# Neighbourhood attention: two heads' value products side by side in the array, and what moves with them

## The chip, the cores and the metric

The kernel runs on one core of a Trainium2 chip. The metric is the device time of one execution in microseconds (us); the kernel before has a median of 3476.13 us over three runs.

## What is computed

Two blocks run one after the other on 512 tokens of width 1024, with a context of 256 tokens. The change touches the first layer of the first block, which is a neighbourhood attention with 16 heads of 64 columns: a grid of 8 rows by 64 columns, where each token looks at a window of 8 by 16 neighbours and at all context tokens. Cut to that part:

```
q, k, v = split(h @ w_qkv)                   # q and k normalised per head
s = concat(q . k_window + bias, q . k_ctx)   # one head, one token
p = softmax(s)
o = p_window . v_window + p_ctx . v_ctx
x = x + g1 * (o @ w_o)                       # g1 and five more rows come from silu(c) @ ada_w + ada_b
x = x + g2 * swiglu(norm(x))                 # the feed-forward stage
```

The tokens of the context go through the same attention over the context alone. The layer after it is a gated scan, and two hybrid layers follow; the change leaves them as they are, except that rows for them are computed during the feed-forward stages.

## The kernel before

**The attention** is `na_heads` (L658). The work on one head is cut into six cells: four of 128 tokens (b = 0 to 3, with 512 scores for each token: 256 from the window, 256 from the context) and two of the context's tokens (b = 4 and 5, 256 scores). A hand-written order, fixed on TensorE (PE) and VectorE (DVE), takes one step g per cell: scores of cell g+1 (`na_scores`, L964), the transposes of the probabilities of cell g-1 (`na_turn`, L1003), the minimum of cell g+1 with the bias added (`na_max`, L981 and L983), its exponential on ScalarE (ACT; `na_exp`, L988), the values of cell g-2 (`na_values`, L1029), the copy of the transposed probabilities of cell g-1 out of PSUM (`na_copy`, L1013 and L1015), and the reciprocal of the sum of cell g+1 (`na_scale`, L994). The store of cell g-3 (`na_store`, L1036) multiplies by that reciprocal on the way from PSUM to `oT`. The cells run head by head: six cells of head 0, then six of head 1.

A value product takes the transposed probabilities `pT` (128 keys by 128 tokens) as the loaded operand and 64 columns of V as the moving one, so that `po` is 128 tokens by 64 columns. It is in float32, and the trace shows two records of PE (and two weight loads, PEld) for each such product. Elsewhere a product is written as three of split parts (`mm3`, L146 to L148), with one record each.

Between the cells PE is fed by a list of units: the projections for Q, K and V (`pacc`), and the transposes that follow for Q and K (`ptq`, L922). The list is paced so that the projections end at step 75 of 96 (`NA_STEPS`). From there to step 95 only the last of the jobs for the modulation rows are left, and this stretch is called the tail here.

**The modulation rows** (`gemv_rows`, L443): each job reads two blocks of `ada_w` (`araw`, 512 KB each) and multiplies them by the two condition vectors in four groups of 32 columns of the array (L464: four products at a time, each with 2 loaded columns, into PSUM rows 0, 32, 64 and 96). ACT copies the sums to `modx` (L468), a DMA of SyncE (SP) then lays the row of biases into partition 2 of `modx` (L469), and a last product with `sel` adds the groups and the bias (L475). The jobs are spread over the list of units; eleven of sixteen end in the tail.

**Behind the loop**, `split_rows` (L938) turns `oT` by 48 transposes on PE (L944), and ACT and DVE write it as a high and a low part, which `out_product` multiplies by `w_o` (`pw`, L146 to L148, 512 columns each). In the function `split_rows` is called for seven of the eight pairs of heads at g = 84 to 90.

**The feed-forward stages** (`ffn`, L286) walk over 22 blocks f. Each has its products (`pau`, `pc`), then silu on ACT, `g` on DVE (L335 and L338), and the parts `gh` on ACT (L341) and `gl` on DVE (L342). After 4, 4, 4, 4, 3 and 3 blocks comes a group of output products (`po`, L146 to L148) which read `gh` and `gl`. Rows for later layers are computed beside it on DVE (`gacc`, L430 to L435, nine long instructions for each vector of a job). There are 24 jobs in each of the two stages, two are begun behind each f, and their instructions are given a late priority, by which a scheduler mixes them into DVE's order.

The order within PE and DVE in the attention loop is the written one; all other engines, and work from outside the loop, are placed by the scheduler where its model has them ready. Every engine runs its queue in order.

Of the kernel before, what the change touches and what calls it, by code (L numbers as in the profile page):

```python
# [284 lines left out]
def ffn(S, l, xs, xout, more):  # L285
# [14 lines left out]
    every = (len(jobs) + 18) // 19  # L300
# [22 lines left out]
    for gi, gn in enumerate(groups):  # L323
        gts = []
        for f in range(f0, f0 + gn):
            pa, pu, *pc = dense(f)
            out_mm = S.lastmm
            g = fp.tile([128, n], F32, name="g", tag="g", bufs=2)
            sa = fp.tile([128, n], F32, name="sa", tag="sa", bufs=2)
            nc.scalar.activation(sa[:, 0:512], pa, AF.Silu)  # L330
            if l == 0:
                gv = g[:, 0:512].rearrange("p (r c) -> p c r", r=ROWS)
                nc.vector.tensor_mul(gv, *[x.rearrange("p (c r) -> p c r", r=ROWS) for x in (sa[:, 0:512], pu)])
            else:
                nc.vector.tensor_mul(g[:, 0:512], sa[:, 0:512], pu)  # L335
            if nt == 6:
                nc.scalar.activation(sa[:, 512:768], pc[0][:, 0:256], AF.Silu)
                nc.vector.tensor_mul(g[:, 512:768], sa[:, 512:768], pc[0][:, 256:512])  # L338
            gh = fp.tile([128, n], F32R, name="gh", tag="gh", bufs=7)
            gl = fp.tile([128, n], F32R, name="gl", tag="gl", bufs=7)  # L340
            nc.scalar.activation(gh, g, AF.Copy)  # L341
            nc.vector.tensor_sub(gl, g, fr(gh))  # L342
            gts.append((gh, gl))
            gemv_flush(S, fp, ps, ("gv", 1), out_mm.ins)
            S.late = late
            for j in jobs[:every]:
                jobs.pop(0)()
# [95 lines left out]
def gemv_rows(S, wname, layer, parts):  # L443
# [9 lines left out]
    sel = S.sb.tile([128, 2], F32, name="sel4")  # L453
    nc.vector.tensor_reduce(sel, S.idf.rearrange("p (j v) -> p v j", j=4)[:, 0:2, :], axis=AX.X, op=OP.add)
    nc.vector.tensor_add(sel, sel, S.idf[:, 2:3].to_broadcast([128, 2]))
    todo = []

    def half(part, c, h):
        S.mark(f"gemv {part}{layer}")
        c0 = PARTS[wname].index(part) * D + c * 256  # L460
        raw = S.gvpool.tile([128, 4, 256], F32, name="araw", tag="araw", bufs=2)
        nc.sync.dma_start(raw, S.wcols(w, c0, 256, 4 * h, 4))
        for k in range(4):
            nc.tensor.matmul(pg[32 * k:32 * k + 2, 0:256], S.cc[:, 4 * h + k, :], raw[:, k, :], start=(h == 0),  # L464
                             stop=(h == 1))
        if h:
            x = S.gvpool.tile([128, 256], F32, name="modx", tag="modx", bufs=1)
            nc.scalar.activation(x, pg[:, 0:256], AF.Copy)  # L468
            nc.sync.dma_start(x[2:3, :], bias[layer:layer + 1, c0:c0 + 256])  # L469
            todo.append((part, c, x))  # L470

    def total():
        part, c, x = todo.pop(0)
        S.mark(f"gemv {part}{layer}")
        nc.tensor.matmul(pg[0:2, 256:512], sel, x, start=True, stop=True)  # L475
# [182 lines left out]
def na_heads(S, na, hT, jobs):  # L658
# [13 lines left out]
    both = na.tile([128, 768], F32, name="bias")  # L672
    nc.gpsimd.memset(both[:, 256:512], 0.0)
# [35 lines left out]
    cells = [(h, b) for h in range(16) for b in range(6)]  # L709
    st = {}  # L710
    fill(NA_HEAD)
    with S.tc.manual_schedule(engines=NA_ENG):
# [8 lines left out]
        for g in range(-1, 100):  # L721
# [3 lines left out]
            if cell(g + 1):  # L725
                h, b = cells[g + 1]
                assert S.nturn[h // 2] == 12, (g, h)
                if b == 0:
                    wide = na.tile([128, 384], F32, name="wide", tag="wide", bufs=2)
                    nc.sync.dma_start(wide, I["rpb_w"][h])  # L730
                    st["wide"] = wide
                st[g + 1] = {}
                na_scores(S, na, st, g + 1, h, b, QK[h // 2][h % 2], mask)
            if cell(g - 3):
# [4 lines left out]
            if cell(g + 1):  # L739
                na_max(S, st[g + 1], *cells[g + 1])  # L740
            upto(g + NA_S[1])
            if cell(g + 1):
                na_exp(S, st[g + 1], *cells[g + 1])
            if cell(g - 2):
                h = cells[g - 2][0]
                assert cells[g - 2][1] or len(V[h // 4][1]) == 3, g
                na_values(S, st[g - 2], *cells[g - 2], V[h // 4])
# [5 lines left out]
            if cell(g + 1):  # L753
                na_scale(S, st[g + 1])
# [181 lines left out]

def split_rows(S, oR, oT, pr):
# [3 lines left out]
    for ts, (hi, lo) in ((range(4), oR.row(pr)), (range(4, 6), oR.crow(pr))):  # L941
        pt = S.acc(128 * len(ts))
        for i, t in enumerate(ts):
            nc.tensor.transpose(pt[:, i * 128:(i + 1) * 128], oT[t][:, pr * 128:(pr + 1) * 128], S.idf)  # L944
        nc.scalar.activation(hi, pt, AF.Copy)
        nc.vector.tensor_sub(lo, pt, fr(hi))


def na_scores(S, na, st, g, h, b, qk, mask):
# [16 lines left out]
    me.update(s=s, p=S.t2("p", n), mx=sb.tile([128, 4], F32, name="mx", tag="mx", bufs=7))  # L966
    if lat:
        if b == 0 or BVAR[b] != BVAR[b - 1]:
            S.bias.reverse()
            o = BOFF[b] * 8  # L970
            nc.gpsimd.tensor_sub(S.bias[0][0], mask[:, BVAR[b], :], st["wide"][:, o:o + 256])
        me["bias"] = S.bias[0][1]
# [18 lines left out]
def na_scale(S, me):  # L991
    S.mark("attscale")
    r = me["mx"][:, 3:4]
    S.nc.vector.reciprocal(r, r)  # L994

# [22 lines left out]
def na_values(S, me, h, b, V):  # L1018
    nc = S.nc
    S.mark(f"att{h}.{b}")  # L1020
    vc = (h % 4) * 64
# [765 lines left out]
```

## Time and profile before

| | us |
|---|---|
| median of three runs | 3476.13 |
| the three runs | 3475.0, 3476.13, 3479.37 |
| the profiled execution | 3472.26 |
| its span | 3470.5 |
| attention loop, projections still running | 109 to 420 of the span |
| the tail | 420 to 521 |
| feed-forward stages | about 600 to 1160, and 1680 to 2060 |

In the rows below PE, PEld, DVE, ACT, POOL and SP are the engines (PEld is PE's weight load). A record's first column is its start in us from the span's start, the second its length; the last bracket tells how long the engine stood idle before it, and what ended that. Ends of PE's records are modelled and overlap, so a product's price is read from one start to the next. PEclk is the clock that the throttle granted to PE, 1.00 being 2.4 GHz and 0.5 being 1.2 GHz.

### The profile page before, as it was taken

The numbers are of one execution on the slowest core, as the hardware profiler recorded it, in microseconds if no ns is written. First come the engines' busy times: TensorE is split into PE (matmuls) and PEld (weight loads), VectorE is DVE, ScalarE is ACT, GpSimd is POOL, SyncE is SP. The second block draws the span as 40 slices with busy tenths as digits, with TensorE's granted clock in tenths as the row PEclk, the third lists the DMA queues.
The fourth block names the chain that finished last, engine by engine and source line by source line (L and its number), as shares of the span: only waits on it lengthen the run. The fifth ranks groups of instructions, "written<-read, shape, count | busy, mean of one in ns | idle before, by whom it ended". The sixth has DMA issues, their size and how long they took to land.

```text
span 3470.5 us, 49643 instructions
## 1 busy us (share of the span) xinstructions
PE 3355.7 (97%) x18924; PEld 2838.8 (82%) x18924; DVE 1892.7 (55%) x3745; ACT 1259.4 (36%) x2480; POOL 720.1 (21%) x650
## 2 busy tenths in 40 slices
PE   7999989999999999999999999999999999999999
PEld 5999857887788788888777878888888788888887
DVE  6456544649864556578778544435552334355523
ACT  4455533222222433334422334333333343333332
POOL 2122202111111211101322223121222221211222
PEclk9999989999999999999999999999999999999999
DMA  6122244324531121111556434232223432322333
GB/s 202 49 75 67 63 135 141 97 67 128 176 116 56 54 62 44 55 49 49 163 165 195 119 108 125 80 104 73 92 78 101 144 104 80 110 69 91 94 97 100
DMA packets 450206, 345.30 MB, mean 99 GB/s; under 512 B 40336, under 2 KB 421552, under 8 KB 449968
## 3 DMA queue, kind: packets, MB, share of 16 engines
q1 hardware_dynamic: 449536, 341.73, 32.9%
q8 instruction: 148, 2.42, 0.3%
q0 software_dynamic: 432, 0.41, 0.1%
q14 instruction: 90, 0.74, 0.1%
HBM read 328.34 MB, written 12.74 MB: 98 GB/s over the span
## 4 chain that ended last, share of the span: by engine, by line
PE 74%; DVE 7%; DMA 2%; ACT 2%; issue 1%; POOL 1%; DVEq 0%; SPq 0%; POOLq 0%; ACTq 0%
PE pacc L148 12%; PE pacc L147 12%; PE pacc L146 12%; PE pau L148 3%; PE pau L146 3%; PE pau L147 3%; PE po L146 3%; PE po L148 3%; PE po L147 3%; PE pw L148 2%; PE pw L146 2%; PE pw L147 2%; DVE gacc L432 2%; PE pl L1194 2%; DVE wlo L135 1%
## 5 line engine op out<-in xcount | busy, mean ns | idle before, releaser
L135 POOL TENSOR_TENSOR wlo<-wraw,whi 128x512 fp32r<-128x512 f32 x388 | 526.7, 1359 | 2121.9 <-ACT whi L132 1762.1
L132 ACT ACTIVATE whi<-wraw 128x512 fp32r<-128x512 f32 x776 | 485.2, 631 | 796.9 <-PE pacc L147 357.8
L135 DVE TENSOR_TENSOR wlo<-wraw,whi 128x512 fp32r<-128x512 f32 x388 | 332.1, 857 | 552.1 <-ACT whi L132 547.4
L148 PE MATMUL pacc<-hT,wlo 128*128 128x512 f32 x1344 | 535.1, 398 | 0.0
L146 PE MATMUL pacc<-hT,whi 128*128 128x512 f32 x1344 | 534.6, 398 | 0.0
L147 PE MATMUL pacc<-hT,whi 128*128 128x512 f32 x1344 | 532.0, 396 | 0.0
L146 PE MATMUL pacc<-whi,hT 128*128 128x256 f32 x1056 | 307.4, 291 | 5.0 <-DVE h L607 2.9
L148 PEld LDWEIGHTS pacc<-hT,wlo 128*128 128x128 f32 x1344 | 252.8, 188 | 58.3
L147 PEld LDWEIGHTS pacc<-hT,whi 128*128 128x128 f32 x1344 | 252.7, 188 | 57.7
L147 PE MATMUL pacc<-wlo,hT 128*128 128x256 f32 x1056 | 299.4, 284 | 0.2 <-DVE wlo L813 0.2
L148 PE MATMUL pacc<-whi,hT 128*128 128x256 f32 x1056 | 298.4, 283 | 0.0
L146 PEld LDWEIGHTS pacc<-hT,whi 128*128 128x128 f32 x1344 | 253.0, 188 | 54.7
L146 PE MATMUL pau<-hT,whi 128*128 128x512 f32 x704 | 280.0, 398 | 0.7 <-DVE h L607 0.7
L148 PE MATMUL pau<-hT,wlo 128*128 128x512 f32 x704 | 280.2, 398 | 0.0
L147 PE MATMUL pau<-hT,whi 128*128 128x512 f32 x704 | 279.1, 396 | 0.0
L432 DVE SCALAR_TENSOR_TENSOR gacc<-araw,cact,gacc 128x256 f32<-128x256 f32 x392 | 222.0, 566 | 23.8 <-DMA araw<-ada_w 10.6
L146 PEld LDWEIGHTS pacc<-whi,hT 128*128 128x128 f32 x1056 | 200.5, 190 | 7.7 <-DVE h L607 3.1
L147 PEld LDWEIGHTS pacc<-wlo,hT 128*128 128x128 f32 x1056 | 200.9, 190 | 2.0 <-DVE wlo L813 0.4
L148 PEld LDWEIGHTS pacc<-whi,hT 128*128 128x128 f32 x1056 | 200.4, 190 | 0.0
L146 PE MATMUL po<-whi,gh 128*128 128x512 f32 x440 | 177.7, 405 | 17.0 <-ACT gh L341 15.7
L147 PE MATMUL po<-wlo,gh 128*128 128x512 f32 x440 | 175.6, 400 | 0.0
L148 PE MATMUL po<-whi,gl 128*128 128x512 f32 x440 | 175.1, 400 | 0.1
(375 smaller groups left out, 6600.4 us busy)
## 6 DMA issues: line engine op xcount, KB each, us to landing
araw<-ada_w SPq DMA_DIRECT2D x96, 512.0 KB
wraw<-w_in SPq DMA_DIRECT2D x96, 512.0 KB
wraw<-ffn_w_in SPq DMA_DIRECT2D x176, 256.0 KB
wraw<-w_in SPq DMA_DIRECT2D x160, 256.0 KB
araw<-w_ada SPq DMA_DIRECT2D x48, 512.0 KB
wraw<-ffn_w_out SPq DMA_DIRECT2D x40, 512.0 KB
x<-x SPq DMA_DIRECT2D x24, 512.0 KB
wraw<-hg_w_in SPq DMA_DIRECT2D x24, 512.0 KB
```

The source lines that it names most:

```text
L132: nc.scalar.activation(hi, r, AF.Copy)
L135: eng.tensor_sub(lo, r, fr(hi))
L146: nc.tensor.matmul(out, lh[0], rh[0], start=first, stop=False)
L147: nc.tensor.matmul(out, lh[0], rh[1], start=False, stop=False)
L148: self.lastmm = nc.tensor.matmul(out, lh[1], rh[0], start=False, stop=last)
L432: nc.vector.scalar_tensor_tensor(acc, r, cv, acc, op0=OP.mult, op1=OP.add)
L1194: nc.tensor.matmul(pl[:, c, :], KX[:, c * 128:(c + 1) * 128], view(Q, c * 128, ([2 * m, 64 // m], [LAT + m, 2], [1, m])), start=True, stop ...
```

## The change

1. `na_values` takes two heads at a time, the same block b of heads 2p and 2p+1. Now 64 columns of V are the loaded operand and `pT` the moving one (128 columns), and the two heads' results go to rows 0 to 63 and 64 to 127 of one `po`. This is called every second step. The result is already turned, so that `split_rows` needs no transposes and no PSUM.
2. Since the tokens are now columns, the division can't be done at the store. `na_scale` multiplies the probabilities themselves, in place, a step later than the reciprocal stood (cell g in step g, behind the minimum of g+1). `na_store` becomes a plain copy of 128 by 128, once for two cells.
3. The cells run in the order head 2p block b, head 2p+1 block b. Each of the two heads has a bias buffer of its own.
4. In `gemv_rows` the bias row goes to partition 98 of `modx`, which ACT's copy (rows 0 to 97) doesn't touch; its DMA is issued before the job's blocks are read.
5. In `ffn` the 24 jobs are spread evenly over 20 of the 22 blocks, instead of two behind each of the first twelve.

```diff
-    every = (len(jobs) + 18) // 19
+    njobs = len(jobs)
...
-            for j in jobs[:every]:
+            while jobs and (njobs - len(jobs)) * 20 < njobs * (f + 1):
                 jobs.pop(0)()
...
+    m = 3 * 32 + 2
...
+        if h == 0:
+            x = S.gvpool.tile([128, 256], F32, name="modx", tag="modx", bufs=1)
+            nc.sync.dma_start(x[m:m + 1, :], bias[layer:layer + 1, c0:c0 + 256])
+            todo.append((part, c, x))
...
         if h:
-            x = S.gvpool.tile([128, 256], F32, name="modx", tag="modx", bufs=1)
-            nc.scalar.activation(x, pg[:, 0:256], AF.Copy)
-            nc.sync.dma_start(x[2:3, :], bias[layer:layer + 1, c0:c0 + 256])
-            todo.append((part, c, x))
+            nc.scalar.activation(todo[0][2][0:m, :], pg[0:m, 0:256], AF.Copy)
...
-        nc.tensor.matmul(pg[0:2, 256:512], sel, x, start=True, stop=True)
+        nc.tensor.matmul(pg[0:2, 256:512], sel[0:m + 1, :], x[0:m + 1, :], start=True, stop=True)
...
-    cells = [(h, b) for h in range(16) for b in range(6)]
+    cells = [(2 * pr + i, b) for pr in range(8) for b in range(6) for i in range(2)]
...
-            if cell(g - 3):
+            if cell(g - 3) and g % 2 == 0:
+                st.pop(g - 4)
                 na_store(S, st.pop(g - 3), *cells[g - 3], oT)
...
                 na_max(S, st[g + 1], *cells[g + 1])
+            if cell(g):
+                na_scale(S, st[g])
...
-            if cell(g - 2):
+            if cell(g - 2) and g % 2:
...
-                na_values(S, st[g - 2], *cells[g - 2], V[h // 4])
+                na_values(S, [st[g - 3], st[g - 2]], *cells[g - 2], V[h // 4])
...
-            if cell(g + 1):
-                na_scale(S, st[g + 1])
...
-    for ts, (hi, lo) in ((range(4), oR.row(pr)), (range(4, 6), oR.crow(pr))):
-        pt = S.acc(128 * len(ts))
-        for i, t in enumerate(ts):
-            nc.tensor.transpose(pt[:, i * 128:(i + 1) * 128], oT[t][:, pr * 128:(pr + 1) * 128], S.idf)
-        nc.scalar.activation(hi, pt, AF.Copy)
-        nc.vector.tensor_sub(lo, pt, fr(hi))
+    for lat, (hi, lo) in ((True, oR.row(pr)), (False, oR.crow(pr))):
+        nc.scalar.activation(hi, o_row(oT, pr, lat), AF.Copy)
+        nc.vector.tensor_sub(lo, o_row(oT, pr, lat), fr(hi))
...
     S.nc.vector.reciprocal(r, r)
+    S.nc.vector.tensor_scalar(p, p, r, None, op0=OP.mult)
...
-    po = S.ps.tile([128, 64], F32, name="po", tag="pv", bufs=1)
+    po = S.ps.tile([128, 128], F32, name="po", tag="pv", bufs=1)
     for j, v in enumerate(vv):
-        nc.tensor.matmul(po, me["pT"][:, j, :], v[:, vc:vc + 64], start=(j == 0), stop=(j == len(vv) - 1))
-    me["po"] = po
+        for i, me in enumerate(two):
+            nc.tensor.matmul(po[64 * i:64 * i + 64, :], v[:, vc + 64 * i:vc + 64 * i + 64], me["pT"][:, j, :],
+                             start=(j == 0), stop=(j == len(vv) - 1))
+    two[1]["po"] = po
...
-    S.nc.vector.tensor_scalar(oT[b][:, h * 64:(h + 1) * 64], me["po"], me["mx"][:, 3:4], None, op0=OP.mult)
+    S.nc.vector.tensor_copy(o_row(oT, h // 2, b < 4)[:, (b % 4) * 128:(b % 4 + 1) * 128], me["po"])
```

PE's queue in the tail, before: `pg<-modx` is the last product of a job, `pg<-araw` one of its two halves, `s`, `pt` and `po` are scores, transposes and values of a cell, and `pacc<-idf,oT` the transposes of `split_rows`.

```order
L944 MATMUL pacc<-idf,oT 128x128 x6
L475 MATMUL pg<-modx,sel_477 2x256
L964 MATMUL s<-qk 128x512 x2
L1003 MATMUL pt<-idf,p 128x128 x4
L464 MATMUL pg<-araw,cc 2x256 x4
L1029 MATMUL po<-v,pT 128x64 x4
L944 MATMUL pacc<-idf,oT 128x128 x6
L964 MATMUL s<-qk 128x256 x2
```

PE's queue in the tail now, some steps before its end:

```order
L971 MATMUL s<-qk 128x512 x2
L1011 MATMUL pt<-idf,p 128x128 x4
L477 MATMUL pg<-modx,sel_477 2x256
L1039 MATMUL po<-pT,vs 64x128 x4
L1039 MATMUL po<-pT,v 64x128 x4
L146 MATMUL pw<-whi,hT 128x512
L147 MATMUL pw<-wlo,hT 128x512
L148 MATMUL pw<-whi,hT 128x512
L146 MATMUL pw<-whi,hT 128x512
L147 MATMUL pw<-wlo,hT 128x512
L469 MATMUL pg<-araw,cc 2x256 x4
```

The transposes of `oT` are gone, eight products of 64 by 128 stand for two cells, and products of `w_o` (`pw`), which before began behind the loop's last cells, stand between the cells: 53 of them ahead of the last values where there were 13.

SP's queue at the same place, before (`row_sc<-modb` stores a finished row):

```order
L478 DMA row_sc_0_482<-modb 2x256
L462 DMA araw<-ada_w 128x4x256
L469 DMA modx<-ada_b 1x256
L462 DMA araw<-ada_w 128x4x256
L478 DMA row_sc_0_482<-modb 2x256
L462 DMA araw<-ada_w 128x4x256 x2
L469 DMA modx<-ada_b 1x256
```

SP's queue now:

```order
L480 DMA row_sc_0_482<-modb 2x256
L467 DMA araw<-ada_w 128x4x256 x2
L464 DMA modx<-ada_b 1x256
L480 DMA row_sc_0_482<-modb 2x256
L467 DMA araw<-ada_w 128x4x256 x2
L464 DMA modx<-ada_b 1x256
L629 DMA x<-x 128x1x1024
```

The DMA of the bias row now stands ahead of the store of the job before, a whole job before its use, and loads of `x` (512 KB) stand among the jobs.

DVE's queue in the second feed-forward stage at the end of a group of blocks, before (`rt` is the first instruction behind an output product):

```order
L430 TENSOR_SCALAR gacc<-araw,cact 128x256
L432 SCALAR_TENSOR_TENSOR gacc<-araw,cact,gacc 128x256 x4
L135 TENSOR_TENSOR wlo<-wraw,whi 128x512
L432 SCALAR_TENSOR_TENSOR gacc<-araw,cact,gacc 128x256 x3
L531 SCALAR_TENSOR_TENSOR modA<-modc,cols 128x8
L335 TENSOR_TENSOR g<-sa,pau 128x512
L435 TENSOR_TENSOR gacc_18651<-gacc,gacc_18651 128x256
L135 TENSOR_TENSOR wlo<-wraw,whi 128x512
L342 TENSOR_TENSOR gl<-g,gh 128x512
L430 TENSOR_SCALAR gacc<-araw,cact 128x256
L432 SCALAR_TENSOR_TENSOR gacc<-araw,cact,gacc 128x256
L539 TENSOR_TENSOR rt<-po,gate 128x512
```

DVE's queue at the end of that group now:

```order
L432 SCALAR_TENSOR_TENSOR gacc<-araw,cact,gacc 128x256 x6
L135 TENSOR_TENSOR wlo<-wraw,whi 128x512
L335 TENSOR_TENSOR g<-sa,pau 128x512
L135 TENSOR_TENSOR wlo<-wraw,whi 128x512
L342 TENSOR_TENSOR gl<-g,gh 128x512
L541 TENSOR_TENSOR rt<-po,gate 128x512
L542 TENSOR_TENSOR x<-x,rt 128x512
```

Ahead of `g` stand fewer instructions of `gacc`, the `modA` that waits for a DMA has moved to a later place, and no `gacc` stands between `g` and `rt`.

## Rows read from the trace of the kernel before

**Rows 1.** The page, part 1: busy time of PE over the whole span.

```profile
PE 3355.7 (97%) x18924; PEld 2838.8 (82%) x18924; DVE 1892.7 (55%) x3745; ACT 1259.4 (36%) x2480; POOL 720.1 (21%) x650
```

**Rows 2.** Busy time by stretch: loop with projections, then the tail.

```profile
core 0: us, PE busy (x) PEld busy (x) DVE busy (x) ACT busy (x) POOL busy (x), PEclk, DMA share, GB/s
...
220.00:320.00 100.00, 98.91 (x838) 92.50 (x836) 59.81 (x168) 51.24 (x135) 21.68 (x24) 1.00 0.23 66
...
420.00:521.00 101.00, 83.59 (x544) 52.17 (x545) 41.23 (x124) 34.17 (x91) 6.61 (x10) 0.81 0.45 128
```

**Rows 3.** The timeline of PE in the loop: the values of one cell.

```profile
305.80 1.00 PE L1029 MATMUL po<-v,pT 128*128 128x64 f32 x8
306.61 0.36 PE L146 MATMUL pacc<-whi,hT 128*128 128x256 f32 x1
306.81 0.28 PE L147 MATMUL pacc<-wlo,hT 128*128 128x256 f32 x1
```

**Rows 4.** The timeline of PE in a later layer: float32 with 128 moving columns.

```profile
2195.11 0.40 PE L148 MATMUL pacc<-hT,wlo 128*128 128x512 f32 x1
2195.35 1.07 PE L1520 MATMUL o<-PT,V 128*128 128x128 f32 x8
2196.26 0.60 PE L1506 MATMUL pt<-idf,P 128*128 128x128 f32 x4
```

**Rows 5.** The timeline of PE in the tail: one product alone, four in column groups.

```profile
491.64 0.59 PE L475 MATMUL pg<-modx,sel 128*2 128x256 f32 x2 [1.29 <-DMA modx<-ada_b]
492.16 1.10 PE L1029 MATMUL po<-v,pT 128*128 128x64 f32 x8
...
495.28 0.61 PE L464 MATMUL pg<-araw,cc 128*2 128x256 f32 x8
495.82 0.66 PE L1029 MATMUL po<-v,pT 128*128 128x64 f32 x4
```

**Rows 6.** By tile: weight loads, shortest/median/longest ns, of 2 and of 128 columns.

```profile
L464 PEld LDWEIGHTS pg<-araw,cc x256: 80/82/85, 185.0 to 510.8; 128*2 128x2 f32 x128
...
L1029 PEld LDWEIGHTS po<-v,pT x512: 186/192/338, 119.3 to 519.0; 128*128 128x128 f32 x171
```

**Rows 7.** Groups by line, 119 to 521 us: transposes of `oT`.

```profile
L944 PE MATMUL pacc<-idf,oT 128*128 128x128 f32 x48 | 7.3, 274 | 0.0
```

**Rows 8.** What PE waited for, 119 to 521 us: total, times, longest.

```profile
PE pg L475 <- DMA modx<-ada_b: 13.0, 8, 3.4
```

**Rows 9.** Busy time by stretch: the tail's first 20 us.

```profile
420.00:440.00 20.00, 17.03 (x80) 10.85 (x80) 7.12 (x22) 6.24 (x17) 1.15 (x2) 0.51 0.26 80
```

**Rows 10.** The timeline of PE in the tail: the two longest of those waits.

```profile
460.22 0.59 PE L475 MATMUL pg<-modx,sel 128*2 128x256 f32 x2 [3.38 <-DMA modx<-ada_b]
...
506.15 1.01 PE L475 MATMUL pg<-modx,sel 128*2 128x256 f32 x2 [2.96 <-DMA modx<-ada_b]
```

**Rows 11.** DVE by line: the store, then multiplications by a column of numbers.

```profile
L1036 DVE TENSOR_SCALAR oT<-po,mx 128x64 f32<-128x64 f32 x96 | 26.3, 274 | 35.2 <-PE po L1029 34.7
...
L1504 DVE TENSOR_SCALAR P<-P,bM 128x256 f32<-128x256 f32 x56 | 17.6, 386 | 0.0
...
L582 DVE TENSOR_SCALAR xn<-x,rr x12: 482/486/1479, 10.5 to 2774.8; 128x512 f32<-128x512 f32 x12
```

**Rows 12.** Busy time by stretch: the loop's ten busiest us of DVE.

```profile
180.00:190.00 10.00, 10.00 (x92) 8.72 (x91) 8.13 (x23) 8.38 (x22) 3.30 (x4) 1.00 0.33 101
```

**Rows 13.** The timeline of PE: three waits at ends of groups of blocks.

```profile
891.79 0.80 PE L146 MATMUL po<-whi,gh 128*128 128x512 f32 x1 [5.80 <-ACT gh L341]
...
1808.68 0.79 PE L146 MATMUL po<-whi,gh 128*128 128x512 f32 x1 [4.53 <-ACT gh L341]
...
1883.05 0.50 PE L146 MATMUL po<-whi,gh 128*128 128x512 f32 x1 [2.59 <-ACT gh L341]
```

**Rows 14.** Busy time by stretch around the first two of them.

```profile
880.00:920.00 40.00, 34.20 (x157) 27.48 (x155) 36.36 (x66) 7.78 (x15) 5.38 (x4) 0.91 0.59 176
...
1800.00:1840.00 40.00, 35.47 (x144) 27.62 (x143) 35.20 (x62) 9.15 (x17) 6.98 (x6) 0.91 0.61 178
```

More of the change, by code (lines that the diff above doesn't have):

```diff
@@ L453, in gemv_rows @@
     sel = S.sb.tile([128, 2], F32, name="sel4")
+    m = 3 * 32 + 2
     nc.vector.tensor_reduce(sel, S.idf.rearrange("p (j v) -> p v j", j=4)[:, 0:2, :], axis=AX.X, op=OP.add)
-    nc.vector.tensor_add(sel, sel, S.idf[:, 2:3].to_broadcast([128, 2]))
+    nc.vector.tensor_add(sel, sel, S.idf[:, m:m + 1].to_broadcast([128, 2]))
     todo = []
@@ L672, in na_heads @@
     both = na.tile([128, 768], F32, name="bias")
+    S.wide = {}
     nc.gpsimd.memset(both[:, 256:512], 0.0)
@@ L728, in na_heads @@
                 if b == 0:
-                    wide = na.tile([128, 384], F32, name="wide", tag="wide", bufs=2)
-                    nc.sync.dma_start(wide, I["rpb_w"][h])
-                    st["wide"] = wide
+                    S.wide[h] = na.tile([128, 384], F32, name="wide", tag="wide", bufs=2)
+                    nc.sync.dma_start(S.wide[h], I["rpb_w"][h])
                 st[g + 1] = {}
                 na_scores(S, na, st, g + 1, h, b, QK[h // 2][h % 2], mask)
-            if cell(g - 3):
+            if cell(g - 3) and g % 2 == 0:
+                st.pop(g - 4)
                 na_store(S, st.pop(g - 3), *cells[g - 3], oT)
@@ L934, in qk_feed, with o_row @@
                 F.then(NA_LAGS[5] + NA_GAP * (2 * u + hh), lambda a=(tt, u, hh): turn(*a), 0.2)
+def o_row(oT, pr, lat):
+    if lat:
+        return oT[pr // 2][:, (pr % 2) * 512:(pr % 2 + 1) * 512]
+    return oT[4 + pr // 4][:, (pr % 4) * 256:(pr % 4 + 1) * 256]
 def split_rows(S, oR, oT, pr):
@@ L965, in na_scores @@
     me = st[g]
-    me.update(s=s, p=S.t2("p", n), mx=sb.tile([128, 4], F32, name="mx", tag="mx", bufs=7))
+    me.update(s=s, p=S.t2("p", n), mx=sb.tile([128, 4], F32, name="mx", tag="mx", bufs=4))
     if lat:
+        bias = S.bias[h % 2]
         if b == 0 or BVAR[b] != BVAR[b - 1]:
-            S.bias.reverse()
             o = BOFF[b] * 8
-            nc.gpsimd.tensor_sub(S.bias[0][0], mask[:, BVAR[b], :], st["wide"][:, o:o + 256])
-        me["bias"] = S.bias[0][1]
+            nc.gpsimd.tensor_sub(bias[0], mask[:, BVAR[b], :], S.wide[h][:, o:o + 256])
+        me["bias"] = bias[1]
 def na_max(S, me, h, b):
@@ L992, in na_scale @@
     S.mark("attscale")
-    r = me["mx"][:, 3:4]
+    p, r = me["p"], me["mx"][:, 3:4]
     S.nc.vector.reciprocal(r, r)
+    S.nc.vector.tensor_scalar(p, p, r, None, op0=OP.mult)
 def na_turn(S, me, h, b):
@@ L1015, in na_copy, with na_values @@
         nc.vector.tensor_copy(pT, pt)
-def na_values(S, me, h, b, V):
+def na_values(S, two, h, b, V):
     nc = S.nc
     S.mark(f"att{h}.{b}")
-    vc = (h % 4) * 64
+    vc = (h % 4 - 1) * 64
     vt, vs = V
```

## The prediction

> **What bounds the kernel now.** I read the page's part 1 first: PE is busy 97% of the span [rows 1], so a change that doesn't shorten PE's own work, or its waits, gains nothing. The averages hide stages, so the second view is the busy time by stretch [rows 2]. In the loop with projections PE is busy 98.9 of 100 us at the full clock: there the price of a PE record is time, and a wait taken from another engine is worth nothing. In the tail PE has 17.4 of 101 us idle and a granted clock of 0.81, that is 19 us lost to the clock if all of it had been work. So the tail is bound by PE's waits and by what the clock does around them, and the third view, PE's waits, names the largest: 13.0 us in eight waits for the DMA of the bias row [rows 8]. In the feed-forward stages the timeline shows PE without gaps but for a few group ends, three of them long [rows 13]; DVE is busy 36.4 and 35.2 of 40 us around the first two [rows 14], so DVE is late there.
>
> **Values, the price on PE.** Today a cell of 128 tokens costs 0.89 us: 0.81 from its start to the next record, and that record lasts 0.20 to its successor instead of some 0.12, which I read as 0.08 still due to the values [rows 3]. That is 0.11 for each of eight records. A record moves only 64 columns here, and with 128 columns moving it costs the same 0.91/8 = 0.11 [rows 4]; so with 64 the loading of 128 columns sets the price, and with 128 both are about equal and the loads are hidden. After the change a record loads 64 columns. A load of 2 columns takes 82 ns and one of 128 takes 192 [rows 6], 0.87 ns a column, so half the load saves some 0.055 us, and 16 loads for two cells cost 16 × 0.055 = 0.89. The moving side is 16 records of 0.11, but the two heads write different columns of the array. Do these run together? Four products in four column groups took 0.54 us, one product of the same moving width alone 0.52 [rows 5]. So column groups do run together, and two cells move in 8 × 0.11 = 0.89. Rows 5 also show a price for going in and out of such a group: 0.52 against 2 × 0.22 for two records of 256 columns at that width's pace leaves about 0.1. I take 1.15 for a pair: 0.89, 0.1 to 0.15 for the change of shape, the rest for loads that don't interleave ideally. Against 1.78 this saves 0.63. A pair of context cells (half the records) goes from 0.89 to 0.70, saving 0.19. With 32 and 16 pairs that is 20.2 + 3.0 = 23.2 us. Bounds: 0.99 a pair (all hidden, one switch) gives 31; streams wholly one after the other, 1.93 a pair, give a loss of 8. I stay near the good end since [rows 5] is the same mechanism on the same engine.
>
> The Trainium skill ("TensorE: Matmul & The Clock Gate", Part 3: Packing small matmuls — row/col tiling, The mechanism) says that a weight load overlaps a running product only when it goes to another group of rows. Here all products use all rows, and by that rule loads and streams would add, to about 1.9 a pair. The trace differs already today: with 128 columns loaded and 128 moving, 0.11 a record leaves no room for both in turn [rows 4].
>
> Three quarters of the pairs (36) lie in the dense loop: 24 × 0.63 + 12 × 0.19 = 17.4. I take off 2 for waits on DVE (next): **15**. The other twelve (eight and four) are worth 5.8 in the tail.
>
> **DVE in the loop.** The scaling adds 64 instructions of 128x512 and 32 of 128x256. The nearest rows are multiplications by a column: 0.482 at 512, 0.386 in place at 256 [rows 11], so 30.8 + 12.4 = 43 us. The stores fall from 96 × 0.274 = 26.3 to 48 copies of twice the width, some 0.3 each, 14.4. Net +31 us, or 0.33 per step. A step of the dense loop is 311/75 = 4.15 us, of which DVE works 60% [rows 2], 2.5; it would work 2.8 of about 3.9. Even its busiest 10 us, 81% [rows 12], stay just under full. The scaling waits for the exponential that was issued a step earlier, and the transposes that read it come a step later. If it waits, the copy of the previous cell's `pT` and the next minimum are queued behind it on DVE, and PE's values behind those. The reciprocal only moves, and the bias buffers by head keep POOL's 48 subtractions the same.
>
> **The tail.** Removed: the 13.0 us of waits [rows 8], since the row's DMA is now issued before the blocks of its own job and behind at most one store on SP. The 48 transposes of `oT` [rows 7] at 0.11 each, the pace of the transposes' four records in [rows 4] as of all others there: 5.3. The values: 5.8. And the half-clock stretches that come behind the longest waits (3.38, 2.96 [rows 10]): the clock of 0.81 stands for some 38 us at half speed, the tail's first 20 are at 0.51 [rows 9] and I leave the start's stretch where it is, some 28 us; of the 10 that I put behind the waits, half is lost time, 5. Together 29. Added: 40 more products of `w_o` run before the last values. At 0.24 [rows 4] they are 9.6 us that only move: the tail gets them, the stage behind it loses them. New waits: with the DMA's waits gone, a step is bound by its chain of scores, minimum, exponential, scaling, transposes, copy and values; PE's own work for a step falls to some 3 us and DVE's is 2 to 3. I put 8 us there (bounds 0 and 25: the second if the tail keeps its idle 17 us and half of the gain of the clock turns over). The high parts of `oT`, now taken straight from SBUF, are ACT's in a stretch where it has two thirds free [rows 2]. `x`'s loads share a DMA that is 45% busy [rows 2]. Sum: 29 − 8 = **21**.
>
> **The feed-forward stages.** Three waits of 5.80, 4.53 and 2.59 us [rows 13] come where DVE has `gacc` work ahead of `g` and `gl`, on which the group's first product waits. Spread over 20 blocks the jobs give 1.2 instead of 2 behind a block, and the order shows the long instructions gone from between `g` and the end. The 12.9 us go but for what a clean end needs (I put 0.6 each): 11. The clock around them is 0.91 over 40 us [rows 14], which is 3.6 us lost, twice; if that stretch is the wait's doing, up to 7 more come back. I take **16** of these 18. Bounds: 22, and nothing, if the later blocks, which had no jobs before, now end late in their place.
>
> **Sum.** 15 + 21 + 16 = 52. Against the profiled execution, 3472.3, that gives 3420; the median is 3.9 above that execution: **3424**.
>
> **The rivals.**
> R1, the change doesn't do what it says: the two halves take turns, 1.93 a pair. Then values cost 8 us more instead of 23 less: 3424 + 31 = 3455. Against it: rows 3 to 5, where loads hide and groups run together. For it: no row shows two groups with weights as wide as 64 columns, and each half's loads come twice as often as a full one's. Chance 0.10. The Trainium skill's rule above would end here.
> R2, the tail is paced by its chain and by the clock: the waits move to the new chain of a step and the clock stays at half, so of the 21 only 4 remain: 3441. For it: a tail with 17% idle at 0.81 is no place where PE's savings are sure, and the scaling adds a link. Against: the products of `w_o` now fill gaps. Chance 0.18.
> R3, slower: DVE becomes the bound in the dense loop. A multiplication at 128x512 has been seen at 1.479 us [rows 11]; if the scaling took that, its mean would be (64 × 1.479 + 32 × 0.386)/96 = 1.1 a step, and if DVE also stood as long before it for the exponential, its step would be 2.5 + 1.1 + 1.5 − 0.1 = 5.0 us, 0.85 above today's 4.15. Over 75 steps 64 us, and no gain there: 3424 + 64 + 15 = 3503. It decides once scaling and its wait add over 1.5 us to a step, for which the median of 0.482 speaks against. Chance 0.04.
> R4: the spread jobs only shift the late ends to other groups, 16 lost: 3440. Chance 0.06.
>
> **How the numbers follow.** My forecast has 0.62, with its own range 3398 to 3440 (the bounds of tail and values, which hardly fall together). R2 and R4 lie at its upper edge, R1 at 3455. To leave out no more than 0.2 the range takes in R1: 3394 to 3457; outside stay R3 and mixtures with two misses or a larger gain. A difference of 0.2%, 7 us, is about what a measurement of this kernel can tell from no change. Faster by more: the forecast, R2, R4 and R1 but for some bad mixtures, 0.92. Within: 0.04. Slower: 0.04, R3.
>
> **What the profile would show.** A pair's values: eight products whose starts span about 1.15 us at full clock; 1.9 is R1. PE's waits for the bias row's DMA gone. In the tail, products of `w_o` among the cells, a clock above 0.81, and waits of PE on DVE under 10 us in all; many of 0.3 us and more on copies of `pT` or on scores' buffers are R2. DVE's scaling at 0.48 and 0.39 us, and DVE below 75% in the dense loop; PE below 97% there is R3. No wait over 2 us at the feed-forward groups, and the granted clock at 1.00 there; otherwise R4. My forecast is wrong most likely in the tail, where a wait and the clock feed each other.

## The result, and the profile after

The changed kernel takes 3431.95 us (median of four runs, 3430.48 to 3433.38), beside 3475.57 for the kernel before in the same measurement: a ratio of 0.9872, with a 95% interval of 0.9855 to 0.9890. It is 43.6 us faster; 52 had been forecast, and the time lies inside the range. The profiled execution has a span of 3428.7 us beside 3470.5, so 41.8 us are to be placed.

A good way to place them is to take instructions that stand in both kernels (the first score, the last value, the first product of a feed-forward stage) and to subtract their starts. The difference is the lead of the changed kernel at that point, and where it moves, time was gained or lost. In this table, worked out from the starts in the traces, the first row gives the start in the kernel before, and the others the lead over it, in us; the experiments' rows are used further down. The 144th score stands near the end of the projections. A single trace is good to a few us only: the changed kernel, e1, e2, e3 and e10 run the same code up to the first feed-forward product, and their leads there lie between 41.1 and 45.0.

| | score 144 | last value | first FFN product, stage 1 | last `pau`, stage 1 | first product of the next layer | first `pau`, stage 2 | last `pau`, stage 2 | end |
|---|---|---|---|---|---|---|---|---|
| before (start) | 398.5 | 519.0 | 590.6 | 1153.5 | 1193.3 | 1685.9 | 2058.8 | 3470.5 |
| changed | 11.1 | 35.5 | 45.0 | 52.4 | 36.3 | 35.4 | 42.4 | 41.8 |
| e1_spread_off | 11.2 | 33.3 | 42.9 | 41.4 | 41.5 | 41.6 | 40.3 | 38.8 |
| e2_late300 | 10.7 | 31.5 | 41.1 | 48.1 | 48.1 | 46.8 | 54.5 | 53.4 |
| e3_spread_14 | 10.5 | 32.5 | 42.0 | 44.3 | 44.4 | 44.4 | 52.2 | 50.6 |
| e4_values_only | 10.8 | 13.6 | 22.9 | 21.9 | 22.0 | 21.7 | 21.0 | 20.8 |
| e5_bias_only | 0.4 | 23.0 | 21.6 | 20.8 | 20.7 | 20.5 | 19.9 | 19.6 |
| e6_split_late | 11.5 | 31.9 | 39.7 | 45.4 | 29.7 | 30.5 | 37.6 | 37.6 |
| e7_noscale | 11.7 | 35.8 | 43.3 | 50.8 | 35.5 | 36.1 | 44.5 | 41.7 |
| e8_serial | -0.8 | 19.7 | 28.9 | 35.8 | 19.6 | 21.6 | 28.8 | 25.9 |
| e9_chunk2 | 9.2 | 31.3 | 40.6 | 45.2 | 29.0 | 29.9 | 36.8 | 35.4 |
| e10_late300_15 | 11.3 | 35.5 | 45.0 | 53.9 | 54.0 | 52.6 | 45.1 | 43.4 |

The changed kernel gains 11 us in the dense loop, 34 in the tail and the stage behind it, 7 in each feed-forward stage, and loses 16 between the first of these and the next layer. That loss was in no step of the forecast.

The page of the changed kernel, busy time over the span, beside [rows 1]:

```profile
PE 3316.9 (97%) x18876; PEld 2792.0 (81%) x18876; DVE 1934.7 (56%) x3807; ACT 1257.1 (37%) x2480; POOL 716.5 (21%) x650
```

Busy time by stretch of the changed kernel: a piece of the dense loop, then the tail from the last product of the projections on, in two parts (columns as in [rows 2]):

```profile
220.00:320.00 100.00, 96.97 (x857) 87.22 (x856) 70.24 (x182) 54.43 (x142) 20.10 (x25) 1.00 0.25 77
403.00:423.00 20.00, 15.43 (x115) 9.38 (x114) 12.46 (x32) 11.47 (x29) 5.13 (x6) 0.83 0.38 113
423.00:484.00 61.00, 55.51 (x448) 29.92 (x445) 39.37 (x111) 22.17 (x60) 4.68 (x6) 1.00 0.75 212
```

In the dense loop DVE went from 60 to 70% and PE from 98.9 to 97.0. The same part of the kernel before, from the last product of its projections to the last value, is

```profile
415.70:519.05 103.35, 84.58 (x561) 53.09 (x560) 41.76 (x128) 35.88 (x96) 9.32 (x12) 0.82 0.44 125
```

So the tail lasts some 80 us instead of 103, PE is idle in 10.1 of them instead of 18.8, and the clock is at half for 7 us in its first 20 and nowhere behind. Its waits, 403 to 484 us of the changed kernel:

```profile
PE pg L469 <- DMA araw<-ada_w: 3.1, 4, 1.1
PE ptq L925 <- DVE cat L915: 2.9, 1, 2.9
PE ptq L925 <- ACT qk L926: 1.3, 2, 0.7
...
PE pt L1011 <- ACT pT L1021: 0.5, 1, 0.5
```

The 13.0 us of [rows 8] are gone, and what is left is small. The values of a pair of 128-token cells, timeline of PE, changed kernel:

```profile
130.98 0.66 PE L1039 MATMUL po<-pT,vs 128*64 128x128 f32 x8
131.47 0.61 PE L1039 MATMUL po<-pT,v 128*64 128x128 f32 x8
132.00 0.38 PE L146 MATMUL pacc<-whi,hT 128*128 128x256 f32 x1
132.22 0.28 PE L147 MATMUL pacc<-wlo,hT 128*128 128x256 f32 x1
```

Sixteen records take 1.02 us, and the record behind lasts 0.22 instead of 0.12: 1.13 in all, where two cells cost 1.78 [rows 3]. Behind a cell of the kernel before that record lasts 0.20, so hardly any of the 0.22 is due to the new shape. All 24 such pairs up to 400 us took 1.02.

The end of the first feed-forward stage is the new place to look at. First DVE there in the changed kernel, then ACT, then PE (the last bracket of a row tells the idle time before it and what ended that):

```profile
1133.89 0.40 DVE L511 TENSOR_TENSOR modrow<-modb,pg 1x256 f32<-1x256 f32 x1
1134.22 0.67 DVE L542 TENSOR_TENSOR x<-x,rt 128x512 f32<-128x512 f32 x1
1135.99 0.41 DVE L511 TENSOR_TENSOR modrow<-modb,pg 1x256 f32<-1x256 f32 x1 [1.10 <-DMA modb<-ada_b]
1138.79 0.41 DVE L511 TENSOR_TENSOR modrow<-modb,pg 1x256 f32<-1x256 f32 x1 [2.39 <-DMA modb<-ada_b]
1152.33 1.53 DVE L609 TENSOR_SCALAR h<-pt,modA,modc 128x512 f32<-128x512 f32 x2 [13.13 <-ACT hT L605]
```

```profile
1140.41 0.63 ACT L168 ACTIVATE xn<-x 128x512 f32<-128x512 f32 x1 [17.95 <-DMA row_g<-modrow]
```

```profile
1136.55 0.77 PE L510 MATMUL pg<-gacc,ones 128*128 128x256 f32 x2 [1.71 <-DVE modrow L511]
1141.80 1.12 PE L600 MATMUL pt<-idf,xn 128*128 128x128 f32 x4 [4.48 <-ACT xn L586]
1144.87 1.11 PE L600 MATMUL pt<-idf,xn 128*128 128x128 f32 x4 [1.95 <-ACT xn L586]
```

The last jobs' rows (`modrow`) are summed behind the stage's last output tile, one after the other, each with a DMA of its bias in front and one of its row behind. The next layer's normalisation, whose scratch `xn` takes memory of the stage that ends (as I read the code), waits 18 us for the store of that last row. Then it has to be done for four tiles with nothing beside it, PE waits 4.5 us for the first and 1.95 for each of the others, and the clock is 0.66 over these 30 us:

```profile
1130.00:1160.00 30.00, 14.27 (x60) 10.44 (x60) 11.96 (x18) 18.01 (x35) 9.09 (x14) 0.66 0.00 1
```

### The profile page after: what moved, and what is told of

Its sections match the earlier page's. It is cut to its first block, busy times and chain, and to the rows that moved or that the text cites. A ratio compares the mean times of both kernels' runs of the same rounds, so it can differ in the third digit from the quotient of the medians.

```text
span 3428.7 us, 49598 instructions
## 1 busy us (share of the span) xinstructions
PE 3316.9 (97%) x18876; PEld 2792.0 (81%) x18876; DVE 1934.7 (56%) x3807; ACT 1257.1 (37%) x2480; POOL 716.5 (21%) x650
## 3 DMA queue, kind: packets, MB, share of 16 engines
q1 hardware_dynamic: 449536, 341.73, 33.3%
## 4 chain that ended last, share of the span: by engine, by line
PE 82%; DVE 9%; DMA 4%; ACT 3%; issue 2%; POOL 1%; SPq 0%; DVEq 0%; POOLq 0%; ACTq 0%
PE pacc L146 15%; PE pacc L148 14%; PE pacc L147 14%; PE pau L148 3%; PE pau L146 3%; PE pau L147 3%; PE po L146 3%; PE po L148 3%; PE po L147 2%; DVE gacc L432 2%; DMA araw<-ada_w 2%; PE pw L148 2%; PE pw L146 2%; PE pw L147 2%; PE pl L1204 2%
```

## The experiments

Theory A for the loss at 1130 us was the late row, with the spread jobs as its cause; the tail's gain had two candidates (the bias row, and the products of `w_o` between the cells); and the dense loop had 7 us to explain between what the values' records gave and what the loop gained.

**e1_spread_off**: the changed kernel without part 5.

```diff
-    njobs = len(jobs)
+    every = (len(jobs) + 18) // 19
...
-            while jobs and (njobs - len(jobs)) * 20 < njobs * (f + 1):
+            for j in jobs[:every]:
```

> The changed kernel (3432.0 us) with part 5 undone: the jobs stand again two behind each of the first twelve blocks. In the trace of the changed kernel, the lead over the kernel before is 45.1 us when the first feed-forward stage begins, rises to 57.5 in it, and falls to 36.6 where the next layer begins, with ScalarE waiting 18.0 us there for the store of a row of the last job; in the second stage it rises by 7. Theory A (the late row costs what spreading gains): about 14 us of gains in the two stages go, and the 21 us at the end of the first come back with them: 3425 to 3430. Theory B (spreading gains its 14 us as forecast, the loss at the first stage's end has to do with the attention's part of the change): 3446.

Measured: 3435.3 us (ratio to before 0.9875, 0.9858 to 0.9892). The number is neither theory's, but the lead is Theory A's: it doesn't fall by 16 behind stage 1, and it doesn't rise in either stage. What I had added up wrongly is the size: the wait costs 16 from the last `pau` to the next layer's first product, not 21, and without part 5 the stages lose 1.5 and 1.3 instead of standing still. So part 5 as written is worth some +14 −16 and the measurement can't tell it from nothing.

**e2_late300**: one number of the changed kernel.

```diff
-    late = (1000, 300)[l]
+    late = (300, 300)[l]
```

> The changed kernel with one number changed: the instructions of the first stage's jobs are put 300 places late instead of 1000, as in the second stage; still spread over 20 blocks. The last row's sum then stands on VectorE ahead of ten of the last output tiles instead of behind them all. Theory A: the wait of 18 us for that row and the slow clock behind it go, the gains of spreading stay: 3411 to 3417. Theory B (it is the jobs in the last blocks that cost, wherever the row stands): 3430 to 3435.

Measured: 3414.95 us, ratio 0.9816 (0.9795 to 0.9837), as Theory A had it. The lead rises by 7 in stage 1 and keeps its 48.1 into the next layer. PE's waits there, 1100 to 1150 us, are down to:

```profile
PE pt L600 <- DVE h L609: 2.1, 2, 1.4
PE pv L147 <- POOL wlo L135: 1.1, 1, 1.1
```

The jobs still stand behind the same 20 blocks, so with these it was where their instructions were queued that cost. Since its interval ends below that of the changed kernel, this is also faster than the changed kernel, and the lowest median found, 1.8% below the kernel before (e3's interval overlaps its).

**e3_spread_14**: the other way to get the row out in time.

```diff
-            while jobs and (njobs - len(jobs)) * 20 < njobs * (f + 1):
+            while jobs and (njobs - len(jobs)) * (14, 20)[l] < njobs * (f + 1):
```

> The changed kernel with the jobs of the first stage spread over 14 blocks instead of 20 (the second stage unchanged). Theory A: no late row, the first stage keeps most of its gain at group ends: 3411 to 3419. Theory B: the loss at the end of the first stage stays: about 3432.

Measured: 3421.0 us, ratio 0.9837 (0.9817 to 0.9858), two us beyond Theory A. The late row is gone here too, with the lateness of 1000 places kept, but stage 1 gains 2.3 us instead of 7: with jobs packed into 14 blocks PE waits again at group ends, here from 545 to 1130 us of this run:

```profile
PE po L146 <- ACT gh L341: 5.7, 6, 2.9
PE pg L510 <- ACT gacc L434: 4.1, 3, 2.9
```

**e4_values_only**: parts 1 to 3 alone, that is e1 with `gemv_rows` as before.

> Parts 1 to 3 alone: the values of two heads side by side, the scaling, the order of cells; bias row (part 4) and feed-forward jobs (part 5) as before. Against the run with part 5 alone undone it lacks part 4. Theory A (the bias row's waits, 13.0 us, and the half clock behind them are worth their 18 us): 3443 to 3449, with the waits for the row's DMA back in the tail. Theory B (products of w_o between the cells hide these waits, or keep the clock up): 3428 to 3434, waits for the DMA below 6 us and the clock in the tail above 0.95.

Measured: 3455.3 us, ratio 0.9933 (0.9914 to 0.9952), 20.0 above e1: Theory A, and more than its 18. The dense loop is unchanged (10.8), the tail gains 2.8 us instead of 22. The waits grew, 403 to 510 us of this run. I put that down to steps that became shorter while the DMA's round trip did not; when these DMAs land isn't in the trace:

```profile
PE pg L475 <- DMA modx<-ada_b: 17.8, 7, 3.8
```

The number is Theory A's, but it doesn't refute the mechanism of Theory B, since products of `w_o` stand between the cells for a part of the tail only. From 420 to 460 us of this run none starts, and there PE has five of the seven waits (12.7 us). From 461.6 to 482.4 us 32 of them start, and PE waits for no bias row and the clock stays full:

```profile
420.00:460.00 40.00, 26.66 (x183) 12.78 (x182) 16.86 (x45) 10.44 (x31) 2.98 (x5) 0.80 0.45 135
461.50:482.50 21.00, 20.95 (x154) 12.38 (x150) 15.32 (x40) 6.51 (x18) 1.88 (x2) 1.00 0.79 210
```

From 482.5 to 498.6 us none starts again, and there the other two waits are (1.34 and 3.75 us).

**e5_bias_only**: the kernel before with `gemv_rows` of the changed kernel, nothing else.

> The kernel before (3475 to 3479 us) with part 4 alone: the bias row's DMA a job earlier. With parts 1 to 3 alone the tail gained 2 us, with part 4 beside them 22. Theory A (the bias row's waits are worth it by themselves): the eight waits of 13.0 us gone, the clock of the tail above 0.9, the last values 14 to 20 us earlier, 3456 to 3464. Theory B (without the products of w_o between the cells PE idles elsewhere in the tail and the clock stays low): last values less than 8 us earlier, clock of the tail below 0.87, 3467 to 3475.

Measured: 3458.2 us beside 3479.9, ratio 0.9946 (0.9925 to 0.9966): Theory A. The last value comes 23.0 us earlier, from 13.0 us of waits. From the 144th score on, PE's idle time falls by 9.9 us (other waits take 3 of the 13), and the time lost to the half clock by 12.4. Both kernels have the same wait of 2.31 us for `cat` at about 422 us, and the half clock sets in at it; over 420 to 460 us this run is at

```profile
420.00:460.00 40.00, 36.19 (x264) 22.50 (x264) 19.57 (x60) 16.29 (x45) 2.80 (x5) 0.87 0.54 164
460.00:500.00 40.00, 36.74 (x285) 25.01 (x284) 22.74 (x66) 18.50 (x48) 5.03 (x5) 1.00 0.66 169
```

where the kernel before had 0.66 over the first 40 us, 0.51 over the first 20 of them [rows 9], and 0.81 over the whole tail [rows 2]. So with part 4 the long stretch at half speed shrinks to about a third. No product of `w_o` starts before 489 us in this run, so these aren't needed for it. The kernel before has two of the bias row's waits inside it (0.71 us at 436.0 and 0.47 at 444.2) and this run none before 441 us; that they hold the clock down is my reading, and no run removed one of them alone. e4 and e5 add up: 20.8 + 19.6 = 40.4 us of lead at the end, beside 38.8 for the two together (e1).

**e6_split_late**: the splits of `oT` behind the loop.

```diff
-            if 84 <= g < 91:
-                split_rows(S, S.oR, oT, g - 84)
...
-    split_rows(S, S.oR, oT, 7)
+    for pr in range(8):
+        split_rows(S, S.oR, oT, pr)
```

> The changed kernel (3432 us) with all eight splits of oT behind the loop, so that no product of w_o can stand between the cells. Theory A (these products only move): the loop's last values 9 us earlier than in the changed kernel, the stage behind it 9 us longer plus a few for the first split, in all 3432 to 3440; the clock of the tail stays above 0.95. Theory B (they fill PE's gaps and keep the clock up): the last values no more than 4 us earlier, the clock of the tail below 0.92, waits of PE on the chain of a cell over 8 us in the tail, in all 3442 to 3455.

Measured: 3437.8 us (3434.7 to 3441.0), a ratio of 0.9875 (0.9846 to 0.9903) beside 0.9872 for the changed kernel: no difference that these runs can tell. The leads (31.9 at the last value, 39.7 at the first feed-forward product) are no more than 1.4 us below those of runs whose loop is that of the changed kernel (31.5 to 35.5, and 41.1 to 45.0).

Nor did the edit do what both theories took for granted. The scheduler placed the splits about where the changed kernel has them (ACT writes the high parts of six pairs at 393 to 405 us in both), and their products among the cells: 46 products of `w_o` still start before the last value, beside 53 in the changed kernel. 36 of them start from 403.8 to 436.4 us, where the changed kernel has four, and none from 437 to 480 us. So the run decides between neither theory, but its two stretches can be compared:

```profile
403.00:436.50 33.50, 30.41 (x246) 18.57 (x244) 23.65 (x63) 17.31 (x47) 6.41 (x7) 1.00 0.44 132
436.50:480.00 43.50, 32.97 (x263) 15.92 (x262) 22.29 (x65) 13.66 (x39) 3.21 (x4) 0.87 0.77 222
```

In the first, with the products, the clock is full. In the second, without them, it is 0.87, and there PE has all its waits for the blocks of `ada_w`, in 403 to 530 us of this run:

```profile
PE pg L469 <- DMA araw<-ada_w: 7.8, 4, 3.4
```

So in this run as in e4 PE waits for the jobs' DMAs where no product of `w_o` stands. What their place among the cells is worth in all, no run shows. Behind the bias row the next DMA that PE waits for is that of the blocks.

**e7_noscale**: the changed kernel without the multiplication by the reciprocal.

```diff
-    S.nc.vector.tensor_scalar(p, p, r, None, op0=OP.mult)
```

> The changed kernel without the multiplication of the probabilities by the reciprocal: the division is left out of what is computed. VectorE loses 45.0 + 14.8 us of work in the attention loop. The values gave 18 us in the dense loop by their records, the loop gained 11.1. Theory A (the 7 us between are VectorE's later work, on which PE waits): the lead over the kernel before at the projections' end rises from 11 to 15 or more, in all 3424 to 3430. Theory B (they are PE's own, from another order of units and changes of shape): lead 10 to 12.5, in all 3429 to 3433.

Measured: 3428.9 us, which Theory A's range holds, but the lead at score 144 is 11.7, Theory B's, and the lead is what the two differ by. 59.8 us of VectorE's work are worth 0.6 us in the dense loop and 3 us in all, which is no more than executions of one kernel differ by.

**e8_serial**: the same products of a pair, one head after the other.

```diff
-    for j, v in enumerate(vv):
-        for i, me in enumerate(two):
+    for i, me in enumerate(two):
+        for j, v in enumerate(vv):
```

> The changed kernel with the same products of a pair in another order: all of one head, then all of the other, instead of by turns. Theory A (the two halves run together only since neighbours in the queue are of different columns): a pair costs 1.7 to 2.0 us instead of 1.13, the dense loop's gain of 11 becomes a loss of 3 to 10, in all 3446 to 3460. Theory B (a head's eight records alone go at half the price since its loads are half as wide, whatever runs beside them): a pair at 1.1 to 1.2, in all 3430 to 3434.

Measured: 3446.2 us (3446.1 to 3446.4), ratio 0.9899 (0.9870 to 0.9928). That interval meets the changed kernel's, but the lead at score 144 is −0.8, where every other run with the new values has 9.2 to 11.7: the dense loop's whole gain is gone, so it hangs on the order of these records. A pair takes 1.51 us, 1.63 with the record behind, which is less than Theory A gave (1.7 to 2.0), as is the loss. The timeline of PE shows why, at the same pair as above (`vs` marks the products with the window's V, `v` those with the context's; each head has four records of `vs` and then four of `v`; rows are sorted by start):

```profile
131.72 0.65 PE L1039 MATMUL po<-pT,vs 128*64 128x128 f32 x4
132.21 0.27 PE L1039 MATMUL po<-pT,v 128*64 128x128 f32 x1
132.22 0.33 PE L1039 MATMUL po<-pT,vs 128*64 128x128 f32 x1
132.32 0.27 PE L1039 MATMUL po<-pT,v 128*64 128x128 f32 x1
132.38 0.27 PE L1039 MATMUL po<-pT,vs 128*64 128x128 f32 x1
...
132.71 0.60 PE L1039 MATMUL po<-pT,v 128*64 128x128 f32 x4
133.23 0.38 PE L146 MATMUL pacc<-whi,hT 128*128 128x256 f32 x1
```

The first head's `vs` run alone (0.49 us for four), then its `v` by turns with the second head's `vs`, then the second head's `v` alone. So a record ran beside one that stood four places ahead of it in the queue, and not beside one eight places ahead.

**e9_chunk2** was to tell whether four places are enough.

```diff
-    for j, v in enumerate(vv):
-        for i, me in enumerate(two):
+    for j0 in range(0, len(vv), 2):
+        for i, me in enumerate(two):
+            for j in (j0, j0 + 1):
```

> The changed kernel with the products of a pair in a third order: four records of one head, four of the other, and so twice. By turns a pair of 128-token cells cost 1.02 us from its first record to the next instruction, all of one head and then the other 1.51; a pair of context cells (four records of each head) cost 0.59 in both orders. Theory A (a product that stands four records further back in PE's queue can still run beside the one in front): 1.02 to 1.10 a pair, 3430 to 3434 in all. Theory B (only the seams between the two heads overlap, so the cost grows with the records between seams): 1.2 to 1.35, 3436 to 3442.

Measured: a pair at 1.07 us, 3434.0 us in all (3431.2 to 3436.9): Theory A. The same pair in PE's timeline:

```profile
131.89 0.66 PE L1040 MATMUL po<-pT,vs 128*64 128x128 f32 x8
132.38 0.66 PE L1040 MATMUL po<-pT,v 128*64 128x128 f32 x8
132.96 0.39 PE L146 MATMUL pacc<-whi,hT 128*128 128x256 f32 x1
```

Four records of one head and four of the other run beside each other nearly as well as by turns; of eight and eight only half does.

**e10_late300_15**: e2 with the second stage's jobs over 15 blocks.

```diff
-            while jobs and (njobs - len(jobs)) * 20 < njobs * (f + 1):
+            while jobs and (njobs - len(jobs)) * (20, 15)[l] < njobs * (f + 1):
```

> The kernel with 300 places of lateness in the first stage (3415 us), and the jobs of the second stage spread over 15 blocks instead of 20. There the second stage's lead rises by 13 us over its first four groups and falls by 5 in its last two, whose blocks had no jobs in the kernel before. Theory A (jobs in the last blocks cost these 5): 3409 to 3412. Theory B (denser jobs make the earlier groups wait, as 14 blocks instead of 20 did in the first stage, which gained 2.3 instead of 7): 3415 to 3420.

Measured: 3431.6 us, ratio 0.9859 (0.9843 to 0.9876), worse than e2 and worse than Theory B had it. Stage 1 keeps its gain (45.0 to 53.9), stage 2 turns 7.7 gained into 7.5 lost. Its waits at group ends, in 1640 to 2040 us of this run, then those of the kernel before in 1670 to 2080 and of the changed kernel in 1640 to 2040:

```profile
PE po L146 <- ACT gh L341: 13.6, 3, 4.7
```

```profile
PE po L146 <- ACT gh L341: 7.1, 2, 4.5
```

```profile
PE po L146 <- ACT gh L341: 3.9, 3, 2.1
```

So 15 blocks are worse than the twelve of the kernel before, too: at 1.6 jobs a block the ends of groups two and three still wait over 4 us each, and a third wait of 4.2 comes at the end of the fourth, which had no jobs before. At 1.2 a block the longest is 2.1. Fewer jobs at the end of a stage don't pay for denser ones before.

## Why the prediction came out as it did

**Values: right, to 0.02 us.** 1.15 and 0.70 a pair were forecast, 1.13 and 0.70 measured, and the reading of [rows 5] (column groups run together) is borne out: e8 takes half of the running side by side away and loses 12 us in the dense loop. The load of 64 columns, worked out from [rows 6] as 55 ns below 192, took 137 ns. R1 fell. By the rule of the Trainium skill that the prediction cites ("TensorE: Matmul & The Clock Gate", Part 3: Packing small matmuls — row/col tiling, The mechanism) a pair would have been about 1.9. Sixteen records in 1.02 us contradict it for halves that differ in columns alone. The order by turns was a condition that I didn't see, and the change happens to write it: that part is luck.

**Dense loop: 11 instead of 15.** Up to score 144 the values' records give 16.8 us of PE's time back. Against that stand 3.1 us more in the projections' records, 1.6 more in the transposes of Q and K, and 1.0 elsewhere, all from one start to the next. Part is waiting: PE is idle in 3.9 us of the loop up to 403 us, in 1.8 up to the same point before. I had taken off 2 us for DVE, and DVE isn't it (e7). What else makes these records slower isn't settled by the runs.

**DVE: mis-sized, without consequence.** The scaling at 128x512 took 0.70 us on average instead of 0.48, 59.8 us in all instead of 43; some 17 us of it came from POOL's work beside it (last section). DVE's share in the dense loop, 70%, is near the forecast since the stores became cheaper as expected (13.7 us). It never bound PE, so R3 fell too, though PE's 96.97% is just under the 97% that was named as its sign: e7 shows that DVE's work isn't the reason.

**Tail and the stage behind it: 34 instead of 21.** The step that failed is the clock's. I left the long half-speed stretch at the tail's start where it was, and gave back 5 us for the dips behind the waits. From the 144th score to the last value PE's records in the kernel before lost 17.0 us to the half clock and those of the changed one 2.6, so 14 came back. Idle time fell from 18.5 to 9.2, by 9 where the forecast had 13 removed and 8 new. What PE does there costs about the same at the full clock: transposes and values gave 14 where 11 were forecast, the products of `w_o` took 12, and the rest 2. That makes 14 + 9 + 14 − 12 − 2 = 23, and 24.4 before rounding, as the table has it. Behind the loop 9.5 came back (the lead rises from 35.5 to 45.0), since those products were done. R2 fell by e5: without the bias row's waits the clock came back.

**Feed-forward: −3 instead of 16.** The waits for `gh` at group ends, of which the forecast took 11 us away, fell from 8.6 us to 2.8 in stage 1 and from 7.1 to 3.9 in stage 2, where one of 2.1 is left. Stage 1 in 590 to 1170 us of the kernel before, then in 545 to 1125 us of the changed kernel, with the largest of the new waits above it:

```profile
PE po L146 <- ACT gh L341: 8.6, 6, 5.8
```

```profile
PE pau L148 <- DVE wlo L135: 4.8, 2, 2.8
PE po L146 <- ACT gh L341: 2.8, 5, 0.6
```

The new waits for `wlo` are in stage 1. In stage 2 the lead rises by 13 us up to the fourth group of blocks and falls by 6 behind it, where there were no jobs before: the bound that the prediction named came true in part. Each stage gained 7, not 8. What the prediction put at nothing is the end of the stage, which took 16 away: I costed the jobs at the group ends from which they were taken, and named as a bound only that later blocks might end late, not that the rows of the last jobs have a reader and a store behind the stage. R4 (16 lost) had the size and not the mechanism. The result of −3 lies below the bounds that I gave (22 to nothing).

So the total is near by luck: errors of +13 in the tail, −19 in the feed-forward stages and −4 in the loop add up to −10.

## What to carry to other kernels

Where the clock is at half in a stretch with waits, cost a wait that is removed at its length, and the clock that the whole stretch has lost as the upper bound of what may come back beside it: here 13.0 us of waits were worth 23 in e5, and 17.8 were worth 20 between e4 and e1. When background work is spread further, follow its last piece to its last DMA and ask what behind the stage stands on that memory or that row; both an earlier place in the queue (e2) and an earlier last block (e3) took the late row away, and the first kept more of the stage's gain (7 us beside 2.3). Two products that fill half the array's columns each are worth writing by turns, or in runs of no more than four records; the same products head by head gave nothing.

## What the runs showed of the hardware

In the changed kernel the scaling took longer when POOL's subtraction of a bias tile ran beside it: 0.98 us instead of 0.49 for 28 of the 64 of 128x512, and 0.84 instead of 0.35 for 7 of the 32 of 128x256. So it is 0.49 us more for either size, a wait and not a slower pace. All 35 long ones start 0.02 us ahead of such a subtraction. Five others overlap one that starts 0.08 us or more behind them, and these took 0.49 or 0.50. No scaling of 128x512 without one beside it is longer than 0.50. Two timelines at the same place, POOL and then DVE:

```profile
300.62 0.68 POOL L978 TENSOR_TENSOR bias<-namask,wide 128x256 f32<-128x256 bf16 x1 [3.80 <-DVE mx L1001]
```

```profile
300.60 0.98 DVE L1002 TENSOR_SCALAR p<-p,mx 128x512 f32<-128x512 f32 x1
303.16 0.49 DVE L1002 TENSOR_SCALAR p<-p,mx 128x512 f32<-128x512 f32 x1
```

The trace has the subtraction released by the reciprocal (L1001) that stands just ahead of the scaling on DVE, so the two meet in 35 of 48 cases. The Trainium skill ("SBUF — State Buffer", SBUF: two separate sides) says that VectorE, in some of its modes, and GpSimd share a pair of ports as an exclusive lock, that the one that starts first gets it, and that the other stands still. The added 0.49 us agrees with the lock; that DVE lost though its records start 0.02 us earlier does not agree with the order. In this kernel that was some 17 us of DVE's time, hidden by PE.

And the half clock lasts very differently behind waits of like length, all for `cat` at the tail's start. Behind the same 2.31 us at 422 us it went on for 27 us in the kernel before (420.5 to 447.8 us), where two waits of 0.71 and 0.47 us followed, and for 10 in e5 (420.7 to 430.9), where none did. Behind 2.89 us it lasted 7 in the changed kernel (409.2 to 416.1). Behind 2.37 us in e6, with products of `w_o` before and behind it, the clock didn't fall at all.
